# Four merge-gate tiles projected behind the indexer and parked in DRAM, and a second room for the inverse's blocks

## The chip, the cores and the metric

The kernel runs as one program on one core of a Trainium2 chip. The metric is the device time of one execution in microseconds (us), lower is better. A core has five engines with a queue of instructions each, and they work side by side: TensorE (PE, matmuls and transposes; its weight loads are shown as PEld), VectorE (DVE), ScalarE (ACT), GpSimd (POOL) and SyncE (SP). SP computes nothing here; it issues transfers between DRAM and the on-chip memories SBUF and PSUM. ACT and POOL issue some as well.

## The reference, cut to what matters

One decoder layer on 512 tokens of width 1024, in float32. A token mixer has two branches, sparse attention (with an indexer that picks the keys) and a gated DeltaNet. Gates computed from the layer's input `h` weight the two branches:

```python
proj = h @ w_in
(q_att, c_kv, q_idx, k_idx, w_idx, qkv, a, b, z, gates) = jnp.split(proj, SPLITS, axis=-1)
...
rel = jax.nn.relu(jnp.einsum('bqhd,bsd->bqhs', qi, k_idx))       # indexer
iscore = jnp.einsum('bqhs,bqh->bqs', rel, wi)
...
sol = lax.linalg.triangular_solve(eye + A, rhs, left_side=True, lower=True, unit_diagonal=True)  # DeltaNet
...
gates = jax.nn.sigmoid(gates)
g_att, g_dn = gates[..., :D_MODEL], gates[..., D_MODEL:]
merged = g_att * (y_att @ w_br_att) + g_dn * (y_dn @ w_br_dn)
return merged @ w_out
```

Behind it stand a layer norm, a mixture of experts (32 experts, the bulk of the weights) and a second layer norm. The gates depend on `h` alone, so they can be worked out at any time after `h` is there; the branch projections depend on the finished branches.

## The kernel before, in words

**Projections.** `w_in` is stored as tiles of 128 output columns (1024 x 128). To keep float32 accuracy each weight tile and each activation is split in a high part and a low part, and `mm3` makes three matmuls of each product: high x high, high x low, low x high. `project(n, i)` is one tile: 8 slices of the contraction, 24 matmuls with 512 columns, named `pj` in the trace (lines 229, 230, 231). The weight split is `split_w`: ACT writes `w_hi` (line 222), and the rest `w_lo` is subtracted (line 225) by POOL in two halves or by DVE in one piece. The list `plan` holds the tiles in the order in which they are projected; each `project` ends with `look_ahead`, which splits the next tile of `plan`. Which engine subtracts is the list `lo_eng`: POOL at first; for seven splits from line 500 on, DVE; and from the merge loop on (`lo_eng[0] = v`) DVE for all.

**Loads.** Raw weights come in pairs of tiles (1 MB, `wr`, line 254) on SP's queue into a pool of three rooms. The same three rooms take the pairs of columns of `w_ada` (1 MB, `wada`, line 202), which `mod_cols` multiplies with the condition vector: two DVE instructions (`junk`, line 205) of 1024 elements a load.

**Order of the work.** The program is written as straight code; a scheduler sorts it into one queue for each engine by program order and by what is ready, and gives out the rooms of the pools. The stages, with the times of the profiled execution: first tiles and keys (to about 75 us); keys' products, latent keys `CKV`, the indexer's queries `QI` and its scores (`pidx` on PE, `rl` on ACT, lines 543 to 551, 134 to 164 us); the inverse of the 32 x 32 diagonal blocks of the DeltaNet's triangular matrices, a chain of 62 DVE instructions (lines 492 and 494, 143 to 197 us) which ends with a copy (line 495) and a transfer to DRAM (`r_dram`, line 497, on POOL's queue). Meanwhile the first Q, V and Z tiles are projected; each goes through a short convolution on ACT and DVE (`conv_silu`, lines 353 to 358). Then come the eight DeltaNet heads (206 to about 385 us). A head loads its inverted blocks from `r_dram` into `BB` (line 668), zeroed before (line 628); its first matmuls are `F` (line 675), then the recurrence; the projections of the next heads' Q, V and Z tiles and of the attention's queries fill PE between. The attention heads follow (to about 507 us), then the merge, 8 rounds `d` of four projections: two gate tiles (`T_G + 2d`, `T_G + 2d + 1`, with a tanh into `gth`), the DeltaNet branch tile and the attention branch tile (`w_br`, 2d + 1 and 2d), whose sums with the gates are made on DVE (lines 874, 875), and the result split again (lines 878, 879). In rounds 1 to 6 `mod_cols` is called three times a round. Ahead of the merge the finished branches are split in `halves` (line 743: `yd_lo`, `ya_lo`). From about 685 us on come the output projection, the router and the experts.

Of the kernel before, what the change touches and what calls it, by code (L numbers as in the profile page):

```python
# [9 lines left out]
F32 = mybir.dt.float32  # L10
# [9 lines left out]
P = 128  # L20
D = 1024
S = 512
H = 8
# [56 lines left out]
def decoder_layer(ctx: ExitStack, tc: tile.TileContext, A, out, dbg=None):  # L80
# [147 lines left out]
    def mm3(o, a, b, start, stop):  # L228
        pe.matmul(o, a[0], b[0], start=start, stop=False)  # L229
        pe.matmul(o, a[0], b[1], start=False, stop=False)  # L230
        pe.matmul(o, a[1], b[0], start=False, stop=stop)  # L231

    raws, pending = {}, {}
    plan = [("w_in", i) for i in range(T_QI + 4)]
    plan += [("w_in", T_QVZ + i) for i in range(3 * H)]
    for h in range(H):
        if h in (0, 3):
            plan.append(("w_ukv", h // 3 * 2))
        plan.append(("w_in", T_QA + h))
    for d in range(KT):  # L240
        plan += [("w_in", T_G + 2 * d), ("w_in", T_G + 2 * d + 1), ("w_br", 2 * d + 1), ("w_br", 2 * d)]
    plan += [("w_out", k) for k in range(2)]

    def raw_of(key, pool_=None):
# [31 lines left out]
    def project(n, i, rhs=None, name="pj", split=None, bank=None, first=0):  # L276

        hi, lo = split or take(n, i)
        o = (bank or pmm)(name)[:, first:]
        r = rhs or (h_hi, h_lo)  # L280
        for k in range(KT):
            mm3(o, (hi[:, k, :], lo[:, k, :]), (r[0][:, k, first:], r[1][:, k, first:]), k == 0, k == KT - 1)
        look_ahead()
        return o

    h_hi = Parts(bigtile("h_hi", F32R), bigtile("h_hi", F32R))
    h_lo = Parts(bigtile("h_lo", F32R), bigtile("h_lo", F32R))
# [249 lines left out]
    for i in range(1, NT):  # L537
        N = (i + 1) * P
        sc = isc[i - 1]
        for h in range(H):  # L540
            o = pb("pidx")
            q = q_st[h % 2][:, h // 2, (i - 1) * P:i * P]
            pe.matmul(o[:, :N], q, k_hi[:, :N], start=True, stop=False)
            pe.matmul(o[:, :N], q, k_lo[:, :N], start=False, stop=True)
            rl = ip.tile([P, S], F32, name="rl", bufs=2)
            s.activation(rl[:, :N], o[:, :N], AF.Relu)
            if h == 0:
                v.tensor_scalar(sc[:, :N - P], rl[:, :N - P], widx[:, i, 0:1], None, op0=OP.mult)
                v.scalar_tensor_tensor(sc[:, N - P:N], rl[:, N - P:N], widx[:, i, 0:1], cfill, op0=OP.mult, op1=OP.add)
            else:  # L550
                v.scalar_tensor_tensor(sc[:, :N], rl[:, :N], widx[:, i, h:h + 1], sc[:, :N],
                                       op0=OP.mult, op1=OP.add)
    idx.close()
    kx.close()

# [68 lines left out]

    qv = {0: queries_values(0)}
    for h in range(H):
        BB = dq.tile([P, NT, 2, P], F32, name="BB", bufs=1)
        (v if h < 2 else g).memset(BB, 0.0)
        done = (h - 1, ou, ssqq, zs) if h else None
        qTh, vTh = qv.pop(h)  # L630
# [230 lines left out]
    for d in range(KT):  # L861
        for j in range(16 + 6 * (d - 1), min(22 + 6 * (d - 1), 48), 2) if 1 <= d <= 6 else ():
            mod_cols(j, ep)
        if d == KT - 2:
            m_rows = mod_rows()
            h2c = first_norm_rows()
        part = [None, None]
        for b in range(2):
            o = project("w_in", T_G + 2 * d + b)
            part[b] = ep.tile([P, S], F32, name="gth", bufs=4)  # L870
            s.activation(part[b], o, AF.Tanh, scale=0.5)
        for b in (1, 0):
            o = project("w_br", 2 * d + b, rhs=ys[b])
            v.scalar_tensor_tensor(part[b], part[b], 1.0, o, op0=OP.add, op1=OP.mult)
        v.tensor_tensor(part[0], part[0], part[1], op=OP.add)
        for t in range(NT):
            x = part[0][:, t * P:(t + 1) * P]
            s.activation(m[t][:, 0, d, :], x, AF.Copy)
            v.tensor_tensor(m[t][:, 1, d, :], x, m[t][:, 0, d, :].bitcast(F32), op=OP.subtract)
# [800 lines left out]
```

## Time and profile before

| | |
|---|---|
| runs | 1253.59, 1252.64, 1248.45 us; median 1252.64 |
| profiled execution: own time | 1250.48 us |
| its span | 1248.8 us (the time from its first to its last instruction) |
| PE busy | 1179.4 us, 94% of the span |
| DVE, ACT, POOL busy | 754.8, 426.4, 219.7 us |
| mean granted clock of TensorE | 0.981 of full speed |

Busy times of the engines overlap. PE's busy share is near the whole, but PE counts as busy also when its clock is low. The profile's clock column gives what the throttle granted; 1.00 is 2.4 GHz and 0.50 is 1.2 GHz, the two levels that there are.

### The profile page before, as it was taken

The page shows a single profiled execution, that of the slowest core. Times are in us where ns is not written, and L with a number is a line of the kernel's source. Part 1 is how long each engine was busy: PE and PEld are TensorE (multiplying, and loading weights), DVE is VectorE, ACT ScalarE, POOL GpSimd, SP SyncE. Part 2 cuts the span into 40 slices and gives each one's busy share as a digit, 9 for nine tenths or more (in the row PEclk, how much of TensorE's full clock was granted, in tenths as well). Part 3 has the DMA queues.
Part 4 walks back from the last instruction along what each step waited for, and adds up shares of the span by engine and source line. Part 5 has one row for each costly group of instructions (what it writes and reads, how often), then busy time and mean ns, then how long its engine had stood idle before and what let it go on. Part 6 is the DMA issues. An engine that isn't in the chain of part 4 may idle for free.

```text
span 1248.8 us, 16358 instructions
## 1 busy us (share of the span) xinstructions
PE 1179.4 (94%) x6062; PEld 806.0 (65%) x6062; DVE 754.8 (60%) x1677; ACT 426.4 (34%) x900; POOL 219.7 (18%) x224
## 2 busy tenths in 40 slices
PE   5997979999999999999999989999999999999995
PEld 3676757778777777788888875544445555555543
DVE  6686895599974746867636775543444343433356
ACT  3353643666465656422223132211111111111112
POOL 6322233334332221000025232000000000000002
PEclk9999998999999999999999979999999999999998
DMA  8624413122211112466545776789999999999992
GB/s 310 231 68 134 121 42 116 56 65 70 72 39 54 49 68 68 154 226 245 218 152 195 286 308 244 303 350 419 421 420 421 421 421 420 420 421 420 421 373 103
DMA packets 76116, 291.85 MB, mean 234 GB/s; under 512 B 19297, under 2 KB 31745, under 8 KB 51458
## 3 DMA queue, kind: packets, MB, share of 16 engines
q1 hardware_dynamic: 58994, 282.47, 57.6%
q10 hardware_dynamic: 16352, 6.16, 2.1%
q0 software_dynamic: 688, 2.15, 0.5%
q8 instruction: 49, 0.80, 0.3%
q14 instruction: 33, 0.27, 0.1%
HBM read 287.05 MB, written 3.70 MB: 233 GB/s over the span
## 4 chain that ended last, share of the span: by engine, by line
PE 78%; DVE 11%; DMA 3%; ACT 2%; issue 2%; POOL 2%; SPq 1%; ACTq 0%; DVEq 0%; POOLq 0%
PE pwg L1269 9%; PE pj L229 9%; PE pj L231 9%; PE pj L230 9%; PE pwu L1269 8%; PE py L1281 8%; PE comb L1184 5%; PE gx L1205 4%; DMA gr<-g_rows 2%; DVE cacc L356 1%; SPq L1106 1%; PE pt L789 1%; POOL w_lo L225 1%; PE po L231 1%; PE po L230 1%
## 5 line engine op out<-in xcount | busy, mean ns | idle before, releaser
L229 PE MATMUL pj<-h_hi,w_hi 128*128 128x512 f32 (+1 forms) x504 | 203.9, 411 | 19.0 <-ACT h_hi L324 11.5
L231 PE MATMUL pj<-h_hi,w_lo 128*128 128x512 f32 (+1 forms) x504 | 204.7, 407 | 2.3 <-POOL w_lo L225 1.9
L230 PE MATMUL pj<-h_lo,w_hi 128*128 128x512 f32 (+1 forms) x504 | 204.2, 405 | 0.6 <-DVE h_lo L325 0.6
L225 POOL TENSOR_TENSOR w_lo<-wr,w_hi 128x512 fp32r<-128x512 f32 x86 | 116.4, 1376 | 180.8 <-ACT w_hi L222 130.2
L222 ACT ACTIVATE w_hi<-wr 128x1024 fp32r<-128x1024 f32 x85 | 89.7, 1057 | 142.4 <-PE pj L230 96.4
L229 PEld LDWEIGHTS pj<-h_hi,w_hi 128*128 128x128 f32 x504 | 97.2, 193 | 40.2 <-ACT h_hi L324 13.9
L1269 PE MATMUL pwg<-wg,xg 128*64 128x512 f32 x512 | 115.2, 595 | 0.0
L1269 PE MATMUL pwu<-wu,xg 128*64 128x512 f32 x512 | 115.2, 592 | 0.0
L231 PEld LDWEIGHTS pj<-h_hi,w_lo 128*128 128x128 f32 x504 | 97.4, 193 | 21.7 <-POOL w_lo L225 2.3
L230 PEld LDWEIGHTS pj<-h_lo,w_hi 128*128 128x128 f32 x504 | 97.4, 193 | 19.6 <-DVE h_lo L325 1.4
L1281 PE MATMUL py<-wd,hbTs 128*64 128x512 f32 x480 | 106.3, 593 | 0.0
L1269 PEld LDWEIGHTS pwu<-wu,xg 128*64 128x64 f32 x512 | 46.7, 137 | 62.9 <-issue 60.6
L1193 DVE TENSOR_TENSOR acc<-acc,comb 128x512 f32<-128x512 f32 (+1 forms) x126 | 77.4, 668 | 11.6 <-PE comb L1184 6.6
L1191 POOL TENSOR_TENSOR acc<-acc,ad 128x256 f32<-128x256 f32 x6 | 4.6, 790 | 450.4 <-PE comb L1184 447.5
L1281 PEld LDWEIGHTS py<-wd,hbTs 128*64 128x64 f32 x480 | 40.0, 137 | 62.9 <-issue 62.9
L1143 DVE SCALAR_TENSOR_TENSOR eth<-eth,pwg 128x512 f32<-128x512 f32 x16 | 11.0, 688 | 112.6 <-ACT eth L1142 112.5
L1269 PEld LDWEIGHTS pwg<-wg,xg 128*64 128x64 f32 x512 | 36.8, 137 | 65.3 <-issue 62.8
L225 DVE TENSOR_TENSOR w_lo<-wr,w_hi 128x1024 fp32r<-128x1024 f32 x42 | 55.0, 1310 | 27.9 <-ACT w_hi L222 27.1
L1162 DVE SCALAR_TENSOR_TENSOR ys<-py,gsl,gt2r 128x512 f32<-128x512 f32 (+1 forms) x34 | 24.3, 718 | 70.0 <-PE py L1281 62.9
L1145 DVE SCALAR_TENSOR_TENSOR hb<-eth,pwu 128x512 f32<-128x512 f32 x16 | 17.3, 1079 | 74.2 <-PE pwu L1269 74.2
L963 ACT ACTIVATE xg<-gx,h2c 128x256 f32<-128x256 f32 x32 | 17.9, 565 | 127.0 <-PE gx L1205 119.2
L356 DVE SCALAR_TENSOR_TENSOR cacc<-pj,convw,cacc 128x509 f32<-128x509 f32 (+2 forms) x72 | 52.3, 739 | 6.9 <-ACT cacc L353 6.5
(490 smaller groups left out, 2302.7 us busy)
## 6 DMA issues: line engine op xcount, KB each, us to landing
wg<-in_w_gate_dram SPq DMA_DIRECT2D x64, 1024.0 KB, 11.9
wu<-in_w_up_dram SPq DMA_DIRECT2D x64, 1024.0 KB, 16.2
wd<-in_w_down_dram SPq DMA_DIRECT2D x60, 1024.0 KB, 13.3
wr<-in_w_in_dram SPq DMA_DIRECT2D x31, 1024.0 KB, 5.1
wada<-in_w_ada_dram SPq DMA_DIRECT2D x23, 1024.0 KB, 5.3
wr<-in_w_br_dram SPq DMA_DIRECT2D x8, 1024.0 KB, 6.4
gr<-g_rows ACTq DMA_DIRECT2D x16, 256.0 KB, 5.1
wr<-in_w_out_dram SPq DMA_DIRECT2D x4, 1024.0 KB, 4.9
```

The costliest lines, as they stand in the source:

```text
L222: s.activation(hi, raw, AF.Copy)
L225: e.tensor_tensor(lo[:, c], raw[:, c], hi[:, c].bitcast(F32), op=OP.subtract)
L229: pe.matmul(o, a[0], b[0], start=start, stop=False)
L230: pe.matmul(o, a[0], b[1], start=False, stop=False)
L231: pe.matmul(o, a[1], b[0], start=False, stop=stop)
L356: v.scalar_tensor_tensor(acc[:, d:], o[:, :S - d], convw[:, ct, i:i + 1], acc[:, d:], op0=OP.mult, op1=OP.add)
L1162: v.scalar_tensor_tensor(ys[:n, :w], py, gs, gt2r[:n, c], op0=OP.mult, op1=OP.mult)
L1184: pe.matmul(o[:, :w], OT[:n, t * P:(t + 1) * P], y, start=(i == 0), stop=(not bias and i == len(parts) - 1))
L1193: v.tensor_tensor(acc[:, t, c], acc[:, t, c], o[:, :w], op=OP.add)
L1205: pe.matmul(o[:, i, :n], hh[:, t, (j + i) * P:(j + i + 1) * P], O[:, t, :n], start=(t == 0 and q == 0), stop=(t == NT - 1 and q == 1))
L1269: done = pe.matmul(o[64 * x:64 * x + 64], xg[:, 4 * i + j, c0 + 64 * x:c0 + 64 * x + 64], ws[x][:, j * FF:(j + 1) * FF], start=(i == 0 and ...
L1281: pe.matmul(py[c][64 * x:64 * x + 64], hT[:, 2 * i + j, 64 * x:64 * x + 64], ws[x][:, j, 512 * c:512 * c + 512], start=(i == 0 and j == 0) ...
```

## The change

`early_gates(n)` names two gate tiles. `work_out_gates`, called for n = 0 and 1 right behind the indexer, projects them, puts the tanh into `gst` (two rooms) and sends the 128 x 512 result to `gate_rows` in DRAM on ACT's queue. These are four of the sixteen gate tiles: the second one of round 0, both of round 1, and the first of round 2. In `plan` they stand ahead of all Q, V and Z tiles. The merge loop loads them from `gate_rows` on SP's queue in place of projecting them. `BB` gets two rooms.

```diff
+    def early_gates(n):
+        return [("w_in", T_G + 1 + 2 * n + i) for i in range(2)]
...
     plan = [("w_in", i) for i in range(T_QI + 4)]
-    plan += [("w_in", T_QVZ + i) for i in range(3 * H)]
+    plan += early_gates(0) + early_gates(1) + [("w_in", T_QVZ + i) for i in range(3 * H)]
...
-        plan += [("w_in", T_G + 2 * d), ("w_in", T_G + 2 * d + 1), ("w_br", 2 * d + 1), ("w_br", 2 * d)]
+        plan += [("w_in", T_G + 2 * d + b) for b in range(2) if not 0 < 2 * d + b < 5]
+        plan += [("w_br", 2 * d + 1), ("w_br", 2 * d)]
...
+    gate_rows = dram.tile([5, P, S], F32, name="gate_rows")
+    def work_out_gates(n, pool_):
+        for _, i in early_gates(n):
+            o = project("w_in", i)
+            x = pool_.tile([P, S], F32, name="gst", bufs=2)
+            s.activation(x, o, AF.Tanh, scale=0.5)
+            s.dma_start(gate_rows[i - T_G], x)
...
+    for i in range(2):
+        work_out_gates(i, ip)
     idx.close()
...
-        BB = dq.tile([P, NT, 2, P], F32, name="BB", bufs=1)
+        BB = dq.tile([P, NT, 2, P], F32, name="BB", bufs=2)
...
         for b in range(2):
-            o = project("w_in", T_G + 2 * d + b)
             part[b] = ep.tile([P, S], F32, name="gth", bufs=4)
-            s.activation(part[b], o, AF.Tanh, scale=0.5)
+            if 0 < 2 * d + b < 5:
+                ld(part[b], gate_rows[2 * d + b])
+            else:
+                s.activation(part[b], project("w_in", T_G + 2 * d + b), AF.Tanh, scale=0.5)
```

The scheduler moves more than these lines say. In the rows of the changed kernel lines from 285 on carry numbers 15 to 19 higher (line 357 is now 372, line 874 is now 893). The first place is ACT's queue at the end of the indexer. Before, the last score `rl` is followed by head 0's `ktail`, one weight split, and the tanh of a convolution (line 357):

```order
L546 ACTIVATE rl<-pidx 128x512 x5
L639 ACTIVATE ktail<-ktr,tail 128x128 x3
L222 ACTIVATE w_hi<-wr 128x1024
L357 ACTIVATE pj<-cacc 128x512
L353 ACTIVATE cacc<-pj,convw 128x512
L357 ACTIVATE pj<-cacc 128x512
L645 ACTIVATE vs<-vtr,vsc_456 128x128 x4
```

Now the gates' tanh (`gst`), their transfers and the splits of the following tiles stand behind the last scores (the last of the four gates in these rows):

```order
L222 ACTIVATE w_hi<-wr 128x1024
L298 ACTIVATE gst<-pj 128x512
L299 DMA gate_rows<-gst 128x512
L222 ACTIVATE w_hi<-wr 128x1024
L368 ACTIVATE cacc<-pj,convw 128x512
L372 ACTIVATE pj<-cacc 128x512
L368 ACTIVATE cacc<-pj,convw 128x512
L656 ACTIVATE ktail<-ktr,tail 128x128 x3
L222 ACTIVATE w_hi<-wr 128x1024
L469 DMA gr<-g_rows 128x4x128
L372 ACTIVATE pj<-cacc 128x512
```

The convolution's tanh, now line 372, waits for the convolution's DVE part (line 356, now 371), and the next weight split stands behind it. On DVE the convolutions of the first Q and V tiles moved to the end of the inverse's chain and behind it: between the chain's start and its closing copy stand 4 instructions of line 356 now, before 12; the two products of line 664, the four of line 660 and the zeroing of the first `BB` moved too, so that 104 instructions stand there in place of 122. The counts of `pj` matmuls ahead of each head's first `F` on PE's queue:

| `pj` ahead of F of head | 0 | 1 | 2 | 3 | 4 | 5 | 6 | 7 |
|---|---|---|---|---|---|---|---|---|
| before | 551 | 577 | 609 | 640 | 702 | 779 | 873 | 917 |
| changed | 561 | 579 | 653 | 730 | 797 | 879 | 968 | 1013 |

The second place is SP's queue from the last loads before the merge to round 3. Before, a pair of gate tiles (`in_w_in`) and a pair of branch tiles (`in_w_br`) go together, with three `wada` loads between the groups:

```order
L254 DMA wr<-in_w_br_dram 128x2x1024
L202 DMA wada<-in_w_ada_dram 128x2x1024
L834 DMA lnc<-in_ln_c_dram 128x16
L837 DMA lnc<-in_ln_dram 128x8 x2
L202 DMA wada<-in_w_ada_dram 128x2x1024 x2
L254 DMA wr<-in_w_in_dram 128x2x1024
L254 DMA wr<-in_w_br_dram 128x2x1024
L202 DMA wada<-in_w_ada_dram 128x2x1024 x3
L254 DMA wr<-in_w_in_dram 128x2x1024
```

Now the loads from `gate_rows` stand among them, and the first `in_w_br` behind the start of the merge (round 2's pair) stands behind three `wada` loads that follow the last of the four gates:

```order
L259 DMA wr<-in_w_br_dram 128x2x1024 x2
L202 DMA wada<-in_w_ada_dram 128x2x1024 x2
L888 DMA gth<-gate_rows 128x512 x3
L851 DMA lnc<-in_ln_c_dram 128x16
L854 DMA lnc<-in_ln_dram 128x8 x2
L202 DMA wada<-in_w_ada_dram 128x2x1024
L259 DMA wr<-in_w_in_dram 128x2x1024
L888 DMA gth<-gate_rows 128x512
L202 DMA wada<-in_w_ada_dram 128x2x1024 x3
L259 DMA wr<-in_w_br_dram 128x2x1024
```

The third place is DVE's queue behind round 1 of the merge: the last `m` row is the end of the split of that round's result. Before, the weight splits of the following tiles stand apart, with `junk` between:

```order
L879 TENSOR_TENSOR m_4959<-gth,m_4959 128x128
L225 TENSOR_TENSOR w_lo<-wr,w_hi 128x1024
L205 SCALAR_TENSOR_TENSOR junk,mod<-wada,cond 128x1024 x2
L207 SCALAR_TENSOR_TENSOR mod<-mod,bada 128x2
L225 TENSOR_TENSOR w_lo<-wr,w_hi 128x1024
L205 SCALAR_TENSOR_TENSOR junk,mod<-wada,cond 128x1024
L874 SCALAR_TENSOR_TENSOR gth<-gth,pj 128x512
```

Now the splits of round 2's two branch tiles stand together behind three `junk`, and nothing of PE's stands between:

```order
L898 TENSOR_TENSOR m_5096<-gth,m_5096 128x128
L205 SCALAR_TENSOR_TENSOR junk,mod<-wada,cond 128x1024
L207 SCALAR_TENSOR_TENSOR mod<-mod,bada 128x2
L205 SCALAR_TENSOR_TENSOR junk,mod<-wada,cond 128x1024 x2
L207 SCALAR_TENSOR_TENSOR mod<-mod,bada 128x2
L225 TENSOR_TENSOR w_lo<-wr,w_hi 128x1024 x2
```

From the first `yd_lo` (line 743, now 760) to that last row DVE's queue of the changed kernel holds 8 `yd_lo`, 5 `ya_lo`, 12 `junk`, 5 `w_lo`, 4 sums of a branch with its gate, 2 sums of the two branches, 8 `m` and 7 `mod`.

## Rows read from the trace of the kernel before

**Rows 1.** The page's 40 slices of the span (31.2 us each): busy tenths of PE and DVE, the granted clock in tenths.

```profile
PE   5997979999999999999999989999999999999995
DVE  6686895599974746867636775543444343433356
PEclk9999998999999999999999979999999999999998
```

**Rows 2.** Busy time of the engines in stretches: the first column is the stretch, then its length, then each engine's busy us (and instructions), the mean granted clock, the DMA share, GB/s.

```profile
160.00:170.00 10.00, 5.16 (x21) 3.87 (x21) 9.79 (x20) 4.83 (x9) 2.67 (x2) 1.00 0.00 1
170.00:180.00 10.00, 8.25 (x37) 6.66 (x38) 9.78 (x23) 3.47 (x14) 0.00 (x0) 0.83 0.36 120
200.00:210.00 10.00, 6.95 (x28) 5.56 (x27) 4.11 (x6) 5.45 (x9) 4.63 (x5) 0.78 0.60 211
210.00:220.00 10.00, 10.00 (x69) 8.24 (x67) 2.58 (x6) 4.74 (x18) 0.87 (x1) 0.88 0.04 7
300.00:350.00 50.00, 48.25 (x274) 38.86 (x273) 49.12 (x123) 27.80 (x74) 19.73 (x17) 1.00 0.25 77
530.00:685.00 155.00, 155.00 (x667) 124.89 (x666) 96.77 (x147) 43.73 (x72) 20.91 (x18) 1.00 0.56 206
```

**Rows 3.** What PE waited for from 150 to 205 us (first row) and from 205 to 400 us (second row): total us, times, longest.

```profile
PE pj L229 <- DVE qT L358: 5.6, 1, 5.6
...
PE F L675 <- DMA BB<-r_dram: 3.0, 1, 3.0
```

**Rows 4.** PE's timeline at 172 us and at 188 us: start, duration, engine, line, operation; in brackets the idle time before and what ended it.

```profile
171.75 0.79 PE L229 MATMUL pj<-h_hi,w_hi 128*128 128x512 f32 x1 [5.59 <-DVE qT L358]
...
174.47 0.55 PE L229 MATMUL pj<-h_hi,w_hi 128*128 128x512 f32 x1
...
187.76 0.40 PE L229 MATMUL pj<-h_hi,w_hi 128*128 128x512 f32 x1
...
189.16 0.40 PE L229 MATMUL pj<-h_hi,w_hi 128*128 128x512 f32 x1
```

**Rows 5.** ACT's, DVE's and POOL's timelines around the end of the inverse.

```profile
197.13 1.12 DVE L495 COPY y<-y 128x1024 f32<-128x1024 f32 x1
...
198.56 0.58 POOL L497 DMA_DIRECT2D r_dram<-y  x1 [4.12 <-DVE y L495]
...
200.57 0.60 ACT L357 ACTIVATE pj<-cacc 128x512 f32<-128x512 f32 x1 [6.96 <-DVE cacc L356]
201.11 1.04 ACT L222 ACTIVATE w_hi<-wr 128x1024 fp32r<-128x1024 f32 x1
```

**Rows 6.** PE's timeline at the first `F` of heads 0, 1 and 7.

```profile
206.17 1.09 PE L675 MATMUL F<-BB,NTm 128*96 128x96 f32 x5 [3.05 <-DMA BB<-r_dram]
223.02 0.84 PE L675 MATMUL F<-BB,NTm 128*96 128x96 f32 x8
373.59 0.58 PE L675 MATMUL F<-BB,NTm 128*96 128x96 f32 x4
```

**Rows 7.** DVE's groups of instructions from 500 to 680 us: line, operation, out<-in, shapes, count, busy us and mean ns of one; idle time before them.

```profile
L225 DVE TENSOR_TENSOR w_lo<-wr,w_hi 128x1024 fp32r<-128x1024 f32 x31 | 41.4, 1334 | 27.4 <-ACT w_hi L222 26.6
L205 DVE SCALAR_TENSOR_TENSOR junk<-wada,cond 128x1024 bf16<-128x1024 f32 x32 | 39.1, 1222 | 7.0 <-DMA wada<-in_w_ada_dram 6.4
L879 DVE TENSOR_TENSOR m<-gth,m 128x128 fp32r<-128x128 f32 x28 | 10.7, 441 | 0.0
L874 DVE SCALAR_TENSOR_TENSOR gth<-gth,pj 128x512 f32<-128x512 f32 x15 | 10.3, 686 | 21.1 <-PE pj L231 21.1
```

**Rows 8.** DVE's timeline at the start of the merge.

```profile
507.40 0.68 DVE L743 TENSOR_TENSOR yd_lo<-y,yd_hi 128x512 fp32r<-128x512 f32 x1
512.18 2.50 DVE L743 TENSOR_TENSOR yd_lo<-y,yd_hi 128x512 fp32r<-128x512 f32 x4
518.08 1.29 DVE L743 TENSOR_TENSOR ya_lo<-ya,ya_hi 128x512 fp32r<-128x512 f32 x2
523.89 0.69 DVE L874 SCALAR_TENSOR_TENSOR gth<-gth,pj 128x512 f32<-128x512 f32 x1 [0.30 <-PE pj L231]
```

**Rows 9.** SP's timeline in the merge (a row with x3 is three loads, the duration from the first to the last), and PE's at the end of round 2 (the last row is the first matmul of round 3).

```profile
521.13 0.37 SPq L254 DMA_DIRECT2D wr<-in_w_in_dram  x1
523.62 0.37 SPq L254 DMA_DIRECT2D wr<-in_w_br_dram  x1
527.57 10.00 SPq L202 DMA_DIRECT2D wada<-in_w_ada_dram  x3
545.19 0.37 SPq L254 DMA_DIRECT2D wr<-in_w_br_dram  x1
...
568.45 0.40 PE L229 MATMUL pj<-h_hi,w_hi 128*128 128x512 f32 x1
```

**Rows 10.** The page's transfers: issues, KB each, median us from issue to landing.

```profile
wr<-in_w_in_dram SPq DMA_DIRECT2D x31, 1024.0 KB, 5.1
wr<-in_w_br_dram SPq DMA_DIRECT2D x8, 1024.0 KB, 6.4
gr<-g_rows ACTq DMA_DIRECT2D x16, 256.0 KB, 5.1
```

## The prediction

> **What bounds the kernel now.** I read the slices first: PE is at 9 tenths in nearly every slice from the second on, and it dips where the indexer and the block inverse run (the sixth slice, 156 to 187 us, has 7) [rows 1]. So a microsecond of PE work costs a microsecond, unless it falls into one of the few holes. Then the stretches: in the merge PE is busy 155.00 of 155 us at a clock of 1.00 [rows 2], and 32 projections at the rhythm below make 179.2 us, about the length of the whole stage: it is bound by PE's matmuls. The holes before it are 4.84 us in 160 to 170, 1.75 in 170 to 180 and 3.05 in 200 to 210 [rows 2]. The waits give them names: 5.6 us for `qT` of a convolution, since DVE is busy with the inverse's chain, and 3.0 us for head 0's `BB`, which comes through DRAM [rows 3]. Behind the first the clock is at its lower level for six matmuls, 171.75 to 174.47 us [rows 4].
>
> **The rhythm.** Six starts from 187.76 to 189.16 us are 0.2333 us each at the high clock; the six from 171.75 to 174.47 are 0.45 [rows 4]. A tile of 24 matmuls is 5.6 us, four tiles 22.4 us.
>
> **Part 1, the work put ahead of the merge: +22.4 us.** The counts of `pj` ahead of `F` grow by 10 for head 0, 2 for head 1, 44 for head 2 and 90 to 100 from head 3 on. So only 10 x 0.233 = 2.3 us of it falls where the holes are; the rest is moved into the heads, since Q, V and Z tiles now come later. Do the heads hide it? From `F` of head 0 at 206.17 to that of head 7 at 373.59 [rows 6] are 167.4 us with 366 `pj` (917 - 551); these take 85.4 us and leave 82.0, that is 11.7 a head. Head 0 alone is 16.85 us with 26 `pj` (6.1): 10.8 left [rows 6]. The rest of a head is as long with few fillers as with many, so each `pj` costs its whole 0.233 us there. PE is busy 48.25 of 50 us in 300 to 350, and DVE 49.12 [rows 2], so neither has room.
>
> **Part 2, the holes before the heads: -6.5 us.** The wait of 5.6 us should go, because gate tiles need no convolution and PE can run them while DVE makes the inverse; with it goes the slow clock behind it, 6 x 0.22 = 1.3 us. That is 6.9. Against it stand two new orders. PE's transposes of head 0's V tile (ahead of its `F`) now wait for a convolution that DVE does at the end of the chain. On ACT a convolution's tanh (line 357, now 372) stands ahead of the next `w_hi`: before, that instruction held ACT idle for 6.96 us, and the split behind it began at 201.11 [rows 5]. DVE itself gains by the move: 8 instructions of line 356 at about 0.74 us and some others leave the chain, against which the chain's lone instructions lose some overlap. So the closing copy (197.13) and `r_dram` (198.56) [rows 5] come earlier by some microseconds, yet PE has 2.3 us more to do before `F`. I take 6.5, near the one wait that has a reason to vanish. The bounds: 0, if the new waits are as long as the old; and 14.7, all three holes (9.64) and the lower clock at 0.83, 0.78 and 0.88 of 10 us each [rows 2], 5.1 us in all.
>
> **The Trainium skill on this.** The wait ahead of line 357 is a queue's head that holds what is behind it. The Trainium skill, Perfetto Trace Analysis, section "Tensor Engine Instruction (MATMUL, LD_WEIGHTS)", says that ACT, DVE and GpSimd are strict first-in-first-out. By that rule all of ACT's work behind that tanh stops; the trace agrees, with 6.96 us. A sum in which this new wait eats the whole gain is the last rival below.
>
> **Part 3, `BB`'s second room: 0.** PE waited for `BB` once, for head 0 [rows 3], whose room was free; heads 1 to 7 show no such wait. The zeroing of later rooms can start earlier, off PE's path. Between 0 and 3.0 us, and I take 0. The gates' four tanh and transfers are off PE's path too: 256 KB land in 5.1 us [rows 10] and are used hundreds of microseconds later.
>
> **Part 4, what the merge gives back: -8.0 us of 22.4.** Round 3 starts at 568.45 [rows 9]; three rounds of 22.4 before that, round 0 starts at 501.2. Four tiles less would put round 3 at 546.0, in times of the kernel before. But the gate tiles were also the cover for DVE and SP, at three places.
> - Round 0: the DeltaNet branch follows gate 0 at once, at 506.8, and would end at 512.4, but needs all eight `yd_lo`. The last of these ends at 512.18 + 2.50 = 514.68 and the last `ya_lo` at 519.37 [rows 8]. The branch's last slice can't start before 514.7, so it ends at 515.1 or so, 2.7 late. The attention branch needs its fourth slice's `ya_lo` at about 518.9 (one `w_lo` of 1.23 behind it now, so a little sooner than 519.37), four slices or 2.8 us from its end: 521.9, another 1.2 late. Sum 3.9.
> - Round 1: its second branch waits for `w_lo`, one DVE piece: 1.2.
> - Round 2: PE reaches its first branch at about 539.9 (521.9, two branches and 1.2, then gate tile 5 of the sixteen). Its raw pair stands on SP behind three `wada`, each of which needs a room that DVE frees with two `junk`. Before, such a group took 10.0 us from 527.57, and the next `wr` of `w_br` went at 545.19 [rows 9]. Without a `w_br` load ahead of the group it starts some 4 us sooner; I put the raw load at 540.4, it lands 5.1 us later [rows 10], and `w_hi` (1.04 [rows 5]) and `w_lo` (1.33 [rows 7]) end at 547.9. That is 8.0 late, and the clock falls once, 1.3.
>
> So 3.9 + 1.2 + 8.0 + 1.3 = 14.4 of 22.4 us are lost and 8.0 stay. From round 3 on the old order is there again. Upper bound: DVE's queue up to those splits holds 12 `junk` at 1.222, 5 `w_lo` at 1.33, 6 sums at 0.69, 13 `yd_lo` and `ya_lo` at 0.63 (2.50 / 4), 8 `m` at 0.38 (10.7 / 28) and 7 small ones [rows 7, 8], 38 us, from 507.40: it can't be through before 545. The first branch of round 2 needs the split before, 543.7; two tiles later are 554.9, a gain of 13.6. Lower bound 3, if one more `wada` cycle (3.3 us) stands in the way and round 3 loses 2 as well.
>
> **Sum.** +22.4 - 6.5 - 8.0 = +7.9 us. On the profiled execution's 1250.48 that is 1258.4; the median of the runs, 1252.64, is 2.2 above that execution, and with it the sum is 1260.5. I predict 1259, and reckon the rivals from 1251.5, the middle of the two. What follows the merge is moved as a whole. In this text 0.5%, 6.3 us, is about what a measurement can tell from no change.
>
> **Rivals.**
> - *The holes take most of it, no change.* If head 0 is not held up by the new orders, 13 of the 14.7 us of Part 2 come back: 22.4 - 13 - 8 = +1, 1253. For it: holes and slow clock are there. Against: 3.0 us of them are the trip of `r_dram`, which stays, and only 10 of 96 matmuls move ahead of head 0.
> - *PE stays dense in the merge, faster.* The price turns at the raw pair of round 2's branches: issued before 531, it lands at 536 and is split when PE comes at 539. Then only 5.1 us are lost, 17.3 come back, and with holes of 11 the sum is 22.4 - 17.3 - 11 = -6, 1246. For it: DVE has idle time in the merge, 97 busy of 155 us [rows 2]. Against: that idle time lies behind round 2, and DVE's own queue is through at 543.7 at the earliest. The Trainium skill, Perfetto Trace Analysis, section "Identifying Performance Opportunities", says that improving a kernel generally means improving its most-contended engine. Taken alone that speaks for this rival, PE being the one; the rows agree that PE is, but not that it stays so with less cover.
> - *Head 0 starts later, much slower.* If ACT's queue, stopped at the convolution's tanh, lets PE run out of split tiles before head 0, the old 5.6 us come back there: Part 2 is 0, Part 4 is 5: 22.4 - 5 = +17, 1269. For it: that wait was 6.96 us before [rows 5]. Against: DVE's chain is shorter.
>
> **Numbers.** Forecast (between +4 and +13 us) 0.50, no change by the holes (-3 to +4) 0.29, dense merge 0.08, head 0 later (over +13) 0.13. Likeliest 1259. For 8 in 10 the range takes the forecast's cases, most of the first rival's and half of the last one's: 1247 to 1269. Slower than 1258.9 are the last rival and about two thirds of the forecast's cases, 0.46; faster than 1246.4 are the dense merge and nothing else, 0.08; 0.46 between.
>
> **What would show it.** `pj` waits for `qT` at 171 gone; `F` of head 0 between 201 and 208; `F` of head 7 about 13 to 20 us later than before; in the merge a PE wait for `yd_lo` or `ya_lo` in round 0 (some 4 us) and one of 5 us or more for `w_hi` or `w_lo` of round 2's first branch, with the clock below 1.00 behind it. The prediction is wrong if the merge shows no wait in round 2, if `F` of head 7 moves by under 8 us, or if a new wait of over 5 us stands ahead of head 0.

## The result and the profile after

The changed kernel takes 1265.91 us (median of 4 runs, 1263.96 to 1267.54), the kernel before 1251.52 (4 runs): the ratio on record is 1.0134, 95% interval 1.0101 to 1.0166 (the two medians alone give 1.0115). So by the medians it is 14.4 us slower, where 7.5 were forecast; 1265.91 lies inside the range. The profiled execution took 1267.54 us, its span is 1265.8.

The same slices as in [rows 1], of the changed kernel:

```profile
PE   5997897999999999989999979999999999999996
DVE  6686895588985556786744875634444242433256
PEclk9998998999999999999999988999999999999997
```

The stretches that answer to [rows 2] (stretch, length, busy us of PE, PEld, DVE, ACT, POOL with counts, granted clock, DMA share, GB/s):

```profile
160.00:170.00 10.00, 8.84 (x37) 6.54 (x36) 9.69 (x18) 3.94 (x6) 2.96 (x3) 1.00 0.44 151
170.00:180.00 10.00, 10.00 (x45) 8.04 (x44) 9.03 (x15) 3.19 (x4) 4.57 (x4) 1.00 0.39 139
190.00:200.00 10.00, 1.50 (x5) 0.99 (x6) 8.27 (x12) 4.50 (x8) 3.49 (x4) 0.63 0.32 121
...
560.00:570.00 10.00, 4.29 (x19) 3.13 (x17) 6.97 (x17) 2.53 (x7) 0.00 (x0) 0.90 0.75 261
570.00:580.00 10.00, 9.88 (x32) 7.44 (x33) 7.52 (x11) 2.04 (x3) 0.00 (x0) 0.76 0.70 265
```

The old holes at 160 to 180 are nearly closed: 1.16 us idle where 6.59 were. But 190 to 200 has a new one of 8.50 us, at a mean clock of 0.63. From 160 us to head 0 PE is idle for 9.7 us in all, as before (9.6). A second new hole, 5.71 us and a low clock behind it, is in the merge. What PE waited for, from 130 to 420 us and from 400 to 720 us:

```profile
PE vtr L659 <- DVE vT L373: 5.8, 2, 5.5
PE yT L606 <- ACT ou L603: 5.2, 3, 2.4
PE pidx L558 <- ACT rl L561: 4.2, 5, 2.4
PE pj L229 <- ACT w_hi L222: 3.1, 1, 3.1
PE FtFtW L692 <- ACT FW L702: 2.1, 1, 2.1
...
PE pj L229 <- ACT w_hi L222: 5.8, 1, 5.8
PE pj L230 <- DVE yd_lo L760: 1.6, 3, 0.9
PE pj L230 <- DVE ya_lo L760: 0.5, 1, 0.5
```

The wait of `pidx` was there before too (4.1 us). Where the new hole at 190 comes from is in ACT's, DVE's and POOL's timelines (start, duration, in brackets the idle time before and what ended it):

```profile
190.07 0.60 ACT L372 ACTIVATE pj<-cacc 128x512 f32<-128x512 f32 x1 [10.14 <-DVE cacc L371]
191.92 1.07 ACT L222 ACTIVATE w_hi<-wr 128x1024 fp32r<-128x1024 f32 x1
...
192.29 1.05 DVE L510 COPY y<-y 128x1024 f32<-128x1024 f32 x1
193.92 3.24 DVE L681 TENSOR_TENSOR qd<-qT,gr 128x384 f32<-128x384 f32 x1
197.08 0.74 DVE L371 SCALAR_TENSOR_TENSOR cacc<-pj,convw,cacc 128x511 f32<-128x511 f32 x1
198.55 0.69 DVE L373 SCALAR_TENSOR_TENSOR vT<-pj,cacc 128x512 f32<-128x512 f32 x1 [0.73 <-ACT pj L372]
...
194.25 2.48 POOL L225 TENSOR_TENSOR w_lo<-wr,w_hi 128x512 fp32r<-128x512 f32 x2
```

ACT stood 10.14 us at the tanh of head 0's Q convolution (before, a like instruction stood 6.96 [rows 5]), and the next weight split came behind it at 191.92; PE waited for that 3.07 us, to 193.04. Then PE waited 5.46 us, to 199.29, for head 0's V convolution, whose last DVE steps stand behind the inverse's closing copy and behind a `qd` of 3.24 us. The closing copy itself came 4.8 us earlier than before (192.29, was 197.13). The zeroing of both rooms of `BB` stands inside the chain in this trace (at 185.27 and 186.50), so the first one did not leave it, as the description of the change has it.

The points at which heads 0, 2 and 7 begin:

```profile
210.21 0.84 PE L692 MATMUL F<-BB,NTm 128*96 128x96 f32 x8
250.07 0.50 PE L692 MATMUL F<-BB,NTm 128*96 128x96 f32 x4
398.47 0.50 PE L692 MATMUL F<-BB,NTm 128*96 128x96 f32 x4
```

Head 0 is 4.0 us later than in [rows 6], with 10 more `pj` (2.3 us) done; head 7 is 24.9 later, with 96 more (22.4). Two marks go through all that follows: the last `T_lo` of the attention on DVE, which stands for the start of the merge, and the last sum of a branch with its gate, which stands for its end. First the pair before, then after:

```profile
505.31 0.69 DVE L791 TENSOR_TENSOR T_lo<-pt,T_hi 128x512 fp32r<-128x512 f32 x1 [0.94 <-ACT T_hi L790]
680.67 0.69 DVE L874 SCALAR_TENSOR_TENSOR gth<-gth,pj 128x512 f32<-128x512 f32 x1 [3.47 <-PE pj L231]
...
530.26 0.69 DVE L808 TENSOR_TENSOR T_lo<-pt,T_hi 128x512 fp32r<-128x512 f32 x1 [0.94 <-ACT T_hi L807]
695.98 0.69 DVE L893 SCALAR_TENSOR_TENSOR gth<-gth,pj 128x512 f32<-128x512 f32 x1 [3.47 <-PE pj L231]
```

The front costs 24.95 us and the merge, 175.36 us long before and 165.72 now, gives back 9.64. At its end the distance to before is 15.3; by the own times of the two profiled executions it is 17.1, by the medians 14.4. The step from 15.3 to 17.1 arises in the router's stage behind the merge, which no kernel here changes; more on it under the runs with two tiles.

### The profile page after: what moved, and what is told of

Same layout as the page of the kernel before. It is cut to its first block, busy times and chain, and to the rows that moved or that the text cites. A ratio compares the mean times of both kernels' runs of the same rounds, so it can differ in the third digit from the quotient of the medians.

```text
span 1265.8 us, 16385 instructions
## 1 busy us (share of the span) xinstructions
PE 1186.6 (94%) x6062; PEld 810.8 (64%) x6062; DVE 753.4 (60%) x1673; ACT 426.1 (34%) x900; POOL 231.8 (18%) x232
## 4 chain that ended last, share of the span: by engine, by line
PE 76%; DVE 12%; DMA 4%; ACT 3%; issue 2%; POOL 1%; SPq 0%; DVEq 0%; ACTq 0%; POOLq 0%
PE pwg L1288 9%; PE py L1300 8%; PE pwu L1288 8%; PE pj L231 8%; PE pj L229 8%; PE pj L230 8%; PE comb L1203 5%; PE gx L1224 4%; DMA wada<-in_w_ada_dram 1%; DMA gr<-g_rows 1%; PE po L231 1%; PE po L230 1%; PE po L229 1%; DVE cacc L371 1%; DVE y L507 1%
## 5 line engine op out<-in xcount | busy, mean ns | idle before, releaser
L229 PE MATMUL pj<-h_hi,w_hi 128*128 128x512 f32 (+1 forms) x504 | 203.8, 411 | 16.1 <-ACT h_hi L339 11.2
L225 POOL TENSOR_TENSOR w_lo<-wr,w_hi 128x512 fp32r<-128x512 f32 x94 | 126.6, 1369 | 204.2 <-ACT w_hi L222 186.3
L1162 DVE SCALAR_TENSOR_TENSOR eth<-eth,pwg 128x512 f32<-128x512 f32 x16 | 11.0, 688 | 112.6 <-ACT eth L1161 112.5
L225 DVE TENSOR_TENSOR w_lo<-wr,w_hi 128x1024 fp32r<-128x1024 f32 x38 | 48.2, 1272 | 27.0 <-ACT w_hi L222 26.7
```

Of the source, the lines that this page charges most:

```text
L225: e.tensor_tensor(lo[:, c], raw[:, c], hi[:, c].bitcast(F32), op=OP.subtract)
```

## The experiments

My theory was that the four tiles cost their full time, or more, where they stand now, that the merge can give back only 10 of 22.4 us since its loads and DVE don't follow, and that the second room for `BB` does nothing. The kernel before has medians of 1248.1 to 1249.2 us in the comparisons with e1 to e12, and 1251.5 in that with the changed kernel. The table has the difference of each to the kernel before in the same comparison, and by the two marks what the front costs and the merge gives back in its profiled execution:

| run | tiles early | median us | to before | ratio, 95% interval | front, us | merge, us |
|---|---|---|---|---|---|---|
| changed kernel | 4 | 1265.91 | +14.4 | 1.0101 to 1.0166 | +25.0 | -9.6 |
| e1 `BB` alone | 0 | 1249.74 | +1.3 | 0.9991 to 1.0032 | +0.5 | 0.1 |
| e2 gates alone | 4 | 1266.13 | +17.7 | 1.0098 to 1.0166 | +24.2 | -10.3 |
| e3 front alone | 4 | 1272.03 | +23.6 | 1.0165 to 1.0229 | +25.2 | 0.0 |
| e4 merge alone | 0 | 1241.02 | -7.5 | 0.9896 to 0.9954 | -1.7 | -10.1 |
| e5 wada late | 4 | 1270.90 | +22.8 | 1.0123 to 1.0225 | +26.0 | -5.8 |
| e6 merge alone, wada late | 0 | 1243.86 | -4.2 | 0.9937 to 0.9992 | -1.9 | -5.9 |
| e7 Q, V first | 4 | 1262.67 | +14.6 | 1.0067 to 1.0162 | +21.5 | -10.5 |
| e8 both edits | 4 | 1263.57 | +15.5 | 1.0078 to 1.0175 | +20.6 | -8.9 |
| e9 four late tiles | 4 | 1262.40 | +14.3 | 1.0095 to 1.0146 | +25.0 | -14.8 |
| e10 two late tiles | 2 | 1247.14 | -1.0 | 0.9974 to 1.0005 | +4.5 | -11.2 |
| e11 two late, Q, V first | 2 | 1243.14 | -5.0 | 0.9945 to 0.9975 | +6.1 | -11.2 |
| e12 selection later | 4 | 1263.49 | +14.3 | 1.0099 to 1.0192 | +24.7 | -11.0 |

The marks come from one profile of each run. e1, e4 and e6 have the same counts of `pj` ahead of every head, and their fronts differ by 2.4 us; a difference of that size between two rows of the column shows nothing.

### Which part of the change, and which stage

e1 is the kernel before with the second room; e2 the changed kernel without it:

```diff
-        BB = dq.tile([P, NT, 2, P], F32, name="BB", bufs=1)
+        BB = dq.tile([P, NT, 2, P], F32, name="BB", bufs=2)
```

> The kernel before with two rooms for BB, and nothing else. Theory (the four tiles cost about 22 to 25 us where they stand now and the merge gives back about 10; BB's room is worth nothing): 1251.5, within 2 us of the kernel before. Rival (the second room brings a zeroing of BB ahead of the inverse's closing copy and moves head 0): slower by 1 to 4 us, with F of head 0 later than 206.2.

> The changed kernel with one room for BB, so the gates' part alone. Theory: as the changed kernel, 1266, within 2 us. Rival (BB's room costs some microseconds in the changed kernel): 1262 to 1264.

`BB`'s room is worth nothing that can be measured, and the gates alone cost what the whole change costs. In e1 `F` of head 0 comes at 209.39 with 4 more `pj`, later than before as the rival had it, but head 7 comes at 374.09 (373.59 before) and the time is the same within its interval. Head 0 waited for `BB` in e1 as in [rows 3]:

```profile
PE F L675 <- DMA BB<-r_dram: 2.7, 1, 2.7
```

In e2 head 0 begins at 203.18 in place of 210.21, and head 7 at 397.80 in place of 398.47. Of the seven microseconds at head 0, 4.7 are 20 `pj` fewer ahead of it (541 in place of 561), which the heads have to do later; the other 2.4 shrink to 0.7 by head 7. So the start of head 0 by itself does not set the time.

e3 and e4 split the gates' part into its two stages:

```diff
# e3: the merge projects all its gate tiles again (plan and loop as before)
-            if 0 < 2 * d + b < 5:
-                ld(part[b], gate_rows[2 * d + b])
-            else:
-                s.activation(part[b], project("w_in", T_G + 2 * d + b), AF.Tanh, scale=0.5)
+            s.activation(part[b], project("w_in", T_G + 2 * d + b), AF.Tanh, scale=0.5)
...
# e4: no early tiles (in plan neither); the merge loads something else
-    for i in range(2):
-        work_out_gates(i, ip)
...
-                ld(part[b], gate_rows[2 * d + b])
+                ld(part[b], A["x"][:P, :S])
```

> The four gate tiles are projected behind the indexer and parked as in the changed kernel, and projected a second time in the merge as before, so it does 96 matmuls more than either. It prices the work ahead of the merge alone. Theory: +24.9 us on the kernel before, 1276, with the first F of head 7 at 398 as in the changed kernel and a merge without waits on PE. Rival (the merge's waits come from where the merge starts, and not from the tiles missing in it): the merge shows the waits for yd_lo and w_hi all the same, and the time is above 1280.

> The merge as in the changed kernel, but the four gate tiles are projected nowhere: the merge loads a piece of x in place of each, so four gates are wrong and 96 matmuls are left out. It prices what the merge gives back, alone. Theory: 9.7 us less than before, 1241.8, with PE waiting 5 to 6 us for w_hi in round 2 as in the changed kernel. Rival (what is lost in the merge is due to DVE work that the early tiles push there): 16 us or more less, 1235, without that wait.

Both came out as the theory said, e3 somewhat lower in time (1272.0, expected 1276), with a front of 25.2 and a merge as long as before. The two effects add up: 23.6 - 7.5 = 16.1, and the gates alone measured 17.7. In e4 the merge waits as in the changed kernel, though its front has no early tile, so these waits belong to the merge itself. PE's waits in e4's merge:

```profile
PE pj L229 <- ACT w_hi L222: 5.1, 1, 5.1
PE pj L230 <- DVE yd_lo L757: 1.6, 3, 0.9
```

### What keeps the merge from giving back 22.4 us

e5 and e6 move the `wada` loads away from rounds 1 and 2:

```diff
-        for j in range(16 + 6 * (d - 1), min(22 + 6 * (d - 1), 48), 2) if 1 <= d <= 6 else ():
+        for j in range(16 + 8 * (d - 3), 24 + 8 * (d - 3), 2) if 3 <= d <= 6 else ():
             mod_cols(j, ep)
```

> The changed kernel with the sixteen loads of wada in rounds 3 to 6 of the merge (four a round) in place of rounds 1 to 6, so that no wada load stands ahead of round 2's branch weights. Theory (the merge keeps only 10 of 22.4 us because those weights come late behind wada): the wait of 5.8 us for w_hi in round 2 and the low clock behind it go, some 8 us less than the changed kernel, 1258; a wait of 1 to 3 us for yd_lo or ya_lo in round 0 stays. Rival (the tiles that are left run into DVE's splits all the same): the wait stays above 3 us and the time above 1262.

> As the run in which the merge gets four gates for nothing (wrong gates, 96 matmuls left out), with the wada loads in rounds 3 to 6. Theory: the merge gives back 17 to 20 of 22.4 us, 1229 to 1232. Rival (late rounds have no room for four wada each): waits in rounds 3 to 6, and no less than 1238.

The first half of the expectation of e5 held and the total did not; e6 came out by its rival (1243.9, no less than 1238). In e5 round 2's wait of 5.8 us is gone, and round 3's last sum comes at 598.20 in place of 606.49. The three rounds behind it give all of that back and more. DVE's sums of a branch with its gate in e5 (each round has two; shown are the second ones of rounds 3, 4 and 5):

```profile
598.20 0.69 DVE L893 SCALAR_TENSOR_TENSOR gth<-gth,pj 128x512 f32<-128x512 f32 x1
...
624.82 0.69 DVE L893 SCALAR_TENSOR_TENSOR gth<-gth,pj 128x512 f32<-128x512 f32 x1
...
651.45 0.69 DVE L893 SCALAR_TENSOR_TENSOR gth<-gth,pj 128x512 f32<-128x512 f32 x1
```

From one row to the next are 26.6 us, with four `wada` loads, where a round with three took 22.4 before: six loads of 1 MB against five, 4.4 to 4.5 us a load each time. SP's queue shows why no load goes sooner: the group of four took 18.8 us to issue.

```profile
603.86 18.79 SPq L202 DMA_DIRECT2D wada<-in_w_ada_dram  x4
623.43 0.37 SPq L259 DMA_DIRECT2D wr<-in_w_in_dram  x1
626.67 0.37 SPq L259 DMA_DIRECT2D wr<-in_w_br_dram  x1
```

From 600 to 626 us SP waited 24.4 us in all: 19.5 for DVE (at `mod`, `w_lo` and `junk`) and 4.9 for landings of `wada`. So the old rounds were bound by PE and, as I read it, nearly as tightly by the loads through three rooms that DVE empties. Whether the rooms or DVE's own pace is the tighter of the two isn't shown; that a fourth room would cure it was not tried.

e9 takes the four tiles from the merge's end instead:

```diff
-        return [("w_in", T_G + 1 + 2 * n + i) for i in range(2)]
+        return [("w_in", T_G + 11 + 2 * n + i) for i in range(2)]
...
-            if 0 < 2 * d + b < 5:
-                ld(part[b], gate_rows[2 * d + b])
+            if 10 < 2 * d + b < 15:
+                ld(part[b], gate_rows[2 * d + b - 11])
```

> As the run with the gates' part alone, but the four early tiles are those of the merge's end (second gate of round 5, both of round 6, first of round 7), where wada loads and splits have run out. What is projected early is as much. Theory (the merge gives back only 10 of 22.4 us in rounds 0 to 2, because three rooms of raw weights and DVE can't follow there; the loads, not the tiles, set the pace): the merge gives back 18 to 22 us, 8 to 12 less than the run with the gates alone, 1254 to 1258, and no PE wait in round 2. Rival (the merge loses cover wherever tiles are taken out): 1263 to 1268, with new waits for w_hi or gth in rounds 5 to 7.

The waits of rounds 0 and 2 are gone, and the merge gives back 14.8 in place of 9.6, but not the 18 to 22 expected, and the time was missed by 4 us. The rival was right in part: a new wait stands in round 7, for `w_lo` on DVE:

```profile
PE pj L231 <- DVE w_lo L225: 4.7, 1, 4.7
...
670.73 0.50 DVE L859 SCALAR_TENSOR_TENSOR h2c<-modc,lnc 128x8 f32<-128x8 f32 x1 [7.37 <-DMA modc<-m_rows]
671.30 10.81 POOL L268 TENSOR_TENSOR wr<-wr,g 128x1024 f32<-128x1024 f32 x4
674.15 3.36 DVE L225 TENSOR_TENSOR w_lo<-wr,w_hi 128x1024 fp32r<-128x1024 f32 x1
```

DVE's queue is held for 7.37 us by a small operation on the norm's rows that come through DRAM; the split stands behind it. Before, the same operation began at 643.56 with no idle time ahead of it.

### What the front costs, and why

e7 puts the gates behind head 0's Q and V tiles (with one room for `BB`):

```diff
-    plan += early_gates(0) + early_gates(1) + [("w_in", T_QVZ + i) for i in range(3 * H)]
+    plan += [("w_in", T_QVZ + i) for i in range(2)] + early_gates(0) + early_gates(1)
+    plan += [("w_in", T_QVZ + i) for i in range(2, 3 * H)]
...
     qv = {0: queries_values(0)}
+    for i in range(2):
+        work_out_gates(i, dq)
```

> The four gate tiles behind the first head's Q and V tiles instead of ahead of them, one room for BB. Theory (the change makes a new hole of 8.5 us at 190 us, as long as the ones it fills, because head 0's two convolutions stand at the end of the inverse's chain): the convolutions are through early, the gate tiles fill both old holes, PE waits less than 3 us between 160 and 205 us, and F of head 7 comes at 386 to 391 instead of 398; 1256 to 1259. Rival (the heads, not the holes, set the pace): F of head 7 stays within 2 us of 398, and the time at 1266.

> The two last edits together. Theory: both gains add up, 1247 to 1251, no different from the kernel before. Rival by which the added PE work can be hidden to the last: under 1243. Rival by which they share a gain: 1256 or more.

The waits for `vT` and for `w_hi` are gone and head 0 begins at 200.79, 9.4 us earlier than in the changed kernel. But head 7 begins at 395.01, only 3.5 earlier, and the time is 1262.7: the theory of this run was wrong in its size. PE's two longest waits in e7 from 130 to 420 us:

```profile
PE yT L605 <- ACT ou L602: 7.0, 3, 3.0
PE F L693 <- DMA BB<-r_dram: 5.3, 1, 5.3
```

Two other waits stand there instead. Head 0 waits 5.3 us for `BB`: the inverse's closing copy comes at 191.62, 5.5 us earlier than before, and `F` 9.2 us behind it (9.0 before), but 547 `pj` ahead of `F`, 4 fewer than before, don't fill PE until then. And the heads wait for `ou`. So taking the new hole away won 3.4 us of the front's 25. e8, with `wada` late as well, gained nothing over e7 (its rival, 1256 or more); its merge gave back 8.9 in place of 10.5, for the reason that e5 shows.

e10 and e11 have two early tiles in place of four, behind the indexer (e10) or behind head 0's Q and V tiles (e11):

```diff
-    plan += early_gates(0) + early_gates(1) + [("w_in", T_QVZ + i) for i in range(3 * H)]
+    plan += early_gates(1) + [("w_in", T_QVZ + i) for i in range(3 * H)]
...
-            if 10 < 2 * d + b < 15:
+            if 12 < 2 * d + b < 15:
```

> Two early tiles in place of four (second gate of round 6, first of round 7), behind the indexer, one room for BB. On PE's queue 30 of the 48 matmuls stand ahead of head 0's F, where it were 10 of 96 with four tiles. Theory (the holes ahead of head 0 have room for one tile or two, and what is beyond pushes the Q, V and Z tiles into the heads, where each costs its time): the merge gives back 10 to 11 us, the front costs 4 to 8, so 2 to 7 us less than the kernel before, 1242 to 1247. Rival (the heads lose by any displaced tile): front cost 12 or more, 1250 or above.

> The same two tiles, behind head 0's Q and V tiles. Theory: head 0's convolutions come early and the two tiles fill the old hole at 166 us; F of head 0 by 210 with 583 pj done; 1241 to 1246. Rival (only the count of displaced tiles matters, not their place): as the run with two tiles behind the indexer, within 2 us.

Two tiles cost 4.5 and 6.1 us in front for 11.2 us of work, and the merge gives all 11.2 back, so at the merge's end e10 is 6.8 us ahead of the kernel before and e11 5.1. e11 is faster than it in the medians too, by 5.0 us with an interval of 0.9945 to 0.9975; e10 is not (0.9974 to 1.0005), just outside what was expected. What parts the two lies behind the merge, in the router's stage with its chain of small steps between DVE and PE. From the last sum to the first combination of the experts' results (`comb`) it takes 114.2 us before, 116.4 in the changed kernel, 116.5 in e10, 111.4 in e11, with the same 631 matmuls. PE is busy with them for 107.0 us in e10 and 104.2 in e11, at a mean clock of 0.94 and 0.97, and idle for 9.5 and 7.2. There PE waits and its clock falls, each time a little differently; first e10, then e11, two stretches of 20 us from 40 us behind the last sum on:

```profile
714.00:734.00 20.00, 15.54 (x128) 14.28 (x129) 14.37 (x36) 7.08 (x7) 4.55 (x2) 0.74 0.52 199
734.00:754.00 20.00, 16.53 (x138) 13.93 (x138) 13.82 (x39) 5.42 (x8) 6.69 (x4) 0.91 0.88 342
...
716.00:736.00 20.00, 16.75 (x146) 14.64 (x146) 16.77 (x47) 7.45 (x7) 6.32 (x3) 0.83 0.63 238
736.00:756.00 20.00, 17.96 (x144) 12.85 (x145) 12.02 (x38) 7.80 (x12) 4.31 (x4) 1.00 0.84 329
```

By time e11 came out as its theory said (1243.1, expected 1241 to 1246) and its rival did not (4.0 us from e10). But by the marks, which leave the router's stage out, e10 is ahead by 1.7 us, less than two like fronts differ; so that the place ahead of or behind the Q and V tiles matters is not shown. What sets the router's stage to 111 or to 117 us was not tried; it took 112.0 in e3 and 112.6 in e12, so a short one does not belong to e11 alone.

By the marks the second pair of tiles costs 20.6 us for 11.2 us of work (25.0 of e9 against 4.5 of e10). In both e10 and e11 PE's queue has 581 to 583 `pj` ahead of head 0, so 30 of the 48 added matmuls stand there. With four tiles the scheduler put 541 to 561 there. In e10 the convolutions of head 0 also stay inside the inverse's chain: 12 instructions of line 371 stand between its start and its closing copy, as 12 of line 356 did before, where the changed kernel has 4. The closing copy comes at 199.52, later than before, and PE, which waits 1.4 us for `vT`, has work until 204.4. Why the scheduler orders two tiles so and four otherwise is open. The points at which heads 0 and 7 begin in e10:

```profile
209.51 1.56 PE L692 MATMUL F<-BB,NTm 128*96 128x96 f32 x8 [5.08 <-DMA BB<-r_dram]
...
377.78 0.50 PE L692 MATMUL F<-BB,NTm 128*96 128x96 f32 x4
```

Not all of the price lies at the hole. The table has the start of a head against that of the kernel before, with 0.2333 us taken off for each `pj` more that is done by then (plus: ahead):

| us ahead, at `F` of head | 0 | 2 | 5 | 7 |
|---|---|---|---|---|
| changed kernel | -1.7 | 2.4 | -4.3 | -2.5 |
| e2 | 0.7 | 3.0 | -6.6 | -1.8 |
| e7 | 4.4 | 5.8 | -3.8 | 1.0 |
| e9 | -0.2 | 2.2 | -7.4 | -2.6 |
| e10 | 3.7 | 4.4 | 2.3 | 7.0 |
| e11 | 2.2 | 3.5 | -0.2 | 5.0 |
| e12 | 1.0 | 3.3 | -1.4 | -6.8 |

Between e9 and e10 are 2.2 us at head 2 and 9.7 at head 5. So most of what the second pair costs beyond its work arises in heads 2 to 5, and not ahead of head 0.

e12 moves the top-k selection on DVE one head later:

```diff
-SELECT_AT = (2, 3, 4)
+SELECT_AT = (3, 4, 5)
```

> The gates' part alone with the top-k selection on DVE one head later (heads 3, 4 and 5 in place of 2, 3 and 4). By the count of pj, the changed kernel is 2.4 us ahead of the kernel before at F of head 2 and 2.5 us behind it at F of head 7, with waits for ou and FW in between while DVE is full. Theory (the Q and V convolutions that the gate tiles push into these heads meet the selection on DVE): the waits for ou shrink from 5 to under 3 us and the merge begins 3 to 5 us earlier than with the gates alone, 1258 to 1262. Rival (DVE is full of the heads' own work, wherever the selection stands): the merge begins within 2 us of the run with the gates alone, 1263 to 1267.

The merge begins at 530.0, 0.5 later than in e2, and the waits for `ou` are as long (7.2, in e2 7.0). So the rival holds: moving the selection does not lower what the front costs. By the table a part of the loss moves with it, to behind head 5, and it is as large at the merge. PE waits for `ou` of ACT, and `ou` in turn for DVE's `rs_y` (5.1 us from 250 to 360 in the changed kernel, 3.2 before). But DVE is no fuller there than before (46.5 us of 50 in 300 to 350, where [rows 2] have 49.1), so a full DVE alone does not explain the loss; its cause stays open.

## Why the prediction was right in its sign and what was mis-sized

**Part 4, the merge, was right.** 8.0 us were forecast to come back, 9.6 did (e4: 10.1). The main mechanism was the one that was worked out. Round 2's raw pair was put at 540.4 in times of the kernel before; it was issued at 564.24, which less the 24.95 of the front is 539.3 (its landing was put at 5.1 us, from the row of the `in_w_in` pairs; that of `in_w_br` has 6.4, and here `w_hi` began 4.7 us behind the issue):

```profile
551.25 8.80 SPq L202 DMA_DIRECT2D wada<-in_w_ada_dram  x3
564.24 0.37 SPq L259 DMA_DIRECT2D wr<-in_w_br_dram  x1
```

The wait was 5.8 us, forecast 8.0, because the first matmul needs `w_hi` alone (it ran at 570.09, or 545.1 in times of before, forecast 547.9 behind `w_lo`). The lower clock behind it (0.76 in 570 to 580) cost 2.4 us there, forecast 1.3. In round 0 PE idled 2.1 us for `yd_lo` and `ya_lo`, forecast 3.9, and in round 1 0.2, forecast 1.2. These add up to 10.5 of the 12.8 us that were lost; the other 2.3 are put down to no wait here, so a part of the close agreement is luck.

**Part 1 was right as an average.** From head 0 to head 7 are 188.26 us with 452 `pj` (105.5 us): 82.8 remain, 11.8 a head, where [rows 6] gave 11.7. The tiles moved into the heads cost their whole time here. As a rule for each head it does not hold: beside their `pj` heads 0 and 1 are shorter than before and heads 2 to 4 longer (the table above), and in e10 heads 0 to 7 take 168.27 us with 384 `pj`, 0.8 more than before with 18 more (4.2 us).

**Part 3 was right**: e1 and e2 show nothing for `BB`'s room.

**Part 2 failed.** It took -6.5 us, and by the count of `pj` head 0 begins 1.7 us behind the kernel before instead (4.04 later, 2.33 of it for 10 more `pj`). With 0.8 more in the seven heads this is the front's +2.5 (24.95 against 22.4). The wait of 5.6 us at 171 did go. But "the one wait that has a reason to vanish" was priced as if nothing took its place, although the two new orders stood in the same paragraph: both cost what their names say, 3.07 us for the split behind the tanh on ACT and 5.46 for the V convolution, with the clock at 0.63 and 0.86 in 190 to 200 and 200 to 210. The sum of idle time up to head 0 did not change. The bound of 0 for Part 2 was wrong as well: no row excluded that the new hole be longer than the old or the clock behind it lower for longer. And the heads lose something besides, though not from their start: by the count of `pj` the changed kernel is 2.4 us ahead of the kernel before at head 2 (250.07, with 44 more) and 2.5 behind at head 7.

The last rival, "head 0 starts later" (1269, chance 0.13), came nearest: ACT's queue, stopped at the tanh, left PE without a split tile, though that is 3.07 us of the new hole and the V convolution is the rest, and its Part 2 of 0 was nearer than -6.5. What it got wrong is the merge, which it priced at 5. The measured +14.4 us lies in its class (over +13) and outside the forecast's own (+4 to +13). Of the signs named ahead, F of head 0 (210.21, named 201 to 208) and of head 7 (24.9 later, named 13 to 20) were missed, and a new wait of over 5 us ahead of head 0, named as a refutation, was there. By it the forecast's step is refuted. That the total stayed in the range is luck: the range took in half of this rival's cases.

## What to carry to other kernels

A hole on the bound engine is filled only by work that its queue really puts there: count the instructions ahead of the point at which the wait ends, and count what is pushed behind it. When fill work goes ahead of work with a chain behind it (here a convolution on a busy DVE), the hole is not filled but moved, and the new wait has to be priced by the old one, not at nothing. Then look at where the pushed work ends: here taking the new hole away (e7) won 3.4 us of the front's 25, since most matmuls were moved into a stage in which PE has little room. Where a stage gives work away, look for what that work covered: here two tiles taken from the merge's quiet end came back whole, four taken from there by two thirds, and four taken from its start by less than half.

## What the runs showed of the hardware

DVE's multiply `qd` took 3.24 us at 193.92 and 0.55 at 209.70 with the same shape. During the first POOL issued its transfer (193.65 to 194.23) and ran its two pieces of `w_lo` (194.25 to 196.73); `qd` ended at 197.16, 0.43 us behind them. In the kernel before, a `qd` at 188.95 took 1.64 us while POOL ran a piece of `w_lo` from 188.78 to 190.18. In e9 a `w_lo` on DVE took 3.36 in place of 1.23 while POOL multiplied weights. The Trainium skill, SBUF — State Buffer, section "SBUF: two separate sides", says that DVE and GpSimd share one pair of ports as an exclusive lock: of a DVE operation with two SBUF inputs and a GpSimd operation that reads SBUF, the one that starts first holds the pair for its whole instruction and the other is blocked. The trace agrees in that DVE's operation ends shortly behind POOL's, with 3.24 against 0.55. In the order it agrees for the `qd` at 188.95; the one at 193.92 began ahead of POOL's `w_lo` by the profile and was held all the same. No run here separated the two engines, so as a cause it is only read from the rows. In front of head 0 it would have cost the V convolution some 2.7 us.
